# The Conformer convolution of a two-block decoder: 31 multiply-adds on VectorE, or matmuls over four shifts of 32 channels

## The chip, the cores and the metric

The kernel runs on one core of a Trainium2 chip, in float32. The metric is the device time of one execution in microseconds (us). TensorE (PE) does the matmuls, VectorE (DVE) and GpSimd (POOL) the elementwise work, ScalarE (ACT) the activations and most evictions, SyncE (SP) issues most of the DMAs from one queue that works in order.

## What is computed

Two blocks follow each other on 512 tokens of width 1024. The first is attention with a gated feed-forward; the second, on 528 rows (16 meta tokens ahead), has a Conformer branch, a bidirectional state-space branch (SSD) and 16 experts that each choose 66 tokens. The change is in the Conformer branch, cut here to what matters:

```python
def depthwise_conv(x, w, b):
    y = lax.conv_general_dilated(x, w[:, None, :].astype(x.dtype), window_strides=(1,), padding='SAME',
                                 dimension_numbers=('NWC', 'WIO', 'NWC'), feature_group_count=x.shape[-1])
    return y + b.astype(x.dtype)
...
        c = conf_a * jax.nn.sigmoid(conf_g)
        c = depthwise_conv(c, w_conf_dw[l], b_conf_dw[l])
        c = jax.nn.silu(layer_norm(c, conf_ln_g[l], conf_ln_b[l]))
        branch_conf = jnp.einsum('btc,cd->btd', c, w_conf_out[l])
```

The kernel of the convolution has 31 taps (`CONF_KERNEL`), each with its own weight for each of the 1024 channels; no channel mixes with another.

## The kernel before

Activations lie transposed: channels on the 128 partitions, the 528 rows along the free axis. A channel tile is 128 channels, so the Conformer branch has 8 of them (`KD`), the SSM input 24 (16 of `ys`, 4 of `Bt`, 4 of `Ct`), the gate `z` 16 and the branch gates 16.

**A linear tile.** `lin2h` makes one tile of 128 output channels in two halves of 264 columns (`HS`). SP loads the 512 KB of weights into `wraw` (L97, 3 buffers), ACT rounds them to `whi` (L107), POOL takes the rest to `wlo` (L108, 2 buffers each), and PE does three products for each of 8 slices of the contraction (L140 to L142): 48 matmuls of 264 columns.

**A Conformer tile.** `conf_tile(m, pl)` is two linear tiles. `gate_half` takes a tanh of the gate into `ct` (L887). `value_half` multiplies it with the value into `rcp`, which has 15 zeros on either side (L894). ACT does the first tap with the bias (L897); the other 30 taps are one `scalar_tensor_tensor` each on DVE, over all 528 columns, each adding to `co` (L900). They are not issued at once but put on the list `later`. The last one writes the tile to DRAM (`cfD`, L902).

**The order.** PE is scheduled by hand: it works in program order. The other engines' orders come from a scheduler. The program interleaves the pieces: for each of the four SSD groups `g`, `ssd_steps(g)` gives 16 steps, each with preparations (`pre`: on ACT, DVE, POOL) and matmuls (`mm`); between the steps stand the linear tiles of a list `fill` (the SSM convolutions of group g+1, z tiles, gate tiles, Conformer tiles by the table `CT`), and after each step `background(NB)` issues 6 taps, those of the SSM convolution first (`soon`, L749), then those of `later`. In the SSD steps `state_mm` (L806) and `y_mm` (L853) are the products, `M` (L830 to L833, 3 buffers for each direction) the decay matrix that `y_mm` waits for, and `row` a row broadcast from DRAM that SP loads (L817).

**After the groups** come the last four z tiles, the rest of `later`, the Conformer tile 7 from another pool (`lw`), five gate tiles, the sum of squares `ysp` with its reciprocal root (`rsqrt_mean`, L150 to L155), gate tile 15, the loads of `cfD` into `cf` (L1016) and the output products of the two branches.

Of the kernel before, what the change touches and what calls it, by code (L numbers as in the profile page):

```python
# [9 lines left out]
F32 = mybir.dt.float32  # L10
# [42 lines left out]
def lay_out_pv():  # L53
    n = 0
    for name, w in (("attn_g", 8), ("ffn_g", 8), ("dqg", 1), ("dkg", 1), ("sublng", 1), ("lam", 4),
                    ("mix_g", 8), ("cw", 248), ("cb", 8), ("lng", 8), ("lnb", 8), ("sw", 168), ("sb", 24),
                    ("dskip", 16), ("ssmg", 16), ("ffng2", 8), ("dtb", 1), ("alog", 1), ("slot", CAP), ("tid", 5)):
        PV[name] = (n, w)
        n += w
    return n  # L60
# [6 lines left out]
def body(ctx, tc, a, out):  # L67
# [58 lines left out]
    def V(name, i=0, n=1):  # L126
        o, w = PV[name]
        return pv[:, o + i:o + i + n]
# [498 lines left out]
    hv = b2p.tile([P, 24 + 248 + 8], F32, name="hv")  # L627
# [76 lines left out]
    pool.tensor_scalar(hv[:, 24:272], V("cw", 0, 248), 0.5, None, ALU.mult)  # L704
    pool.tensor_scalar(hv[:, 272:], V("lnb", 0, 8), 0.5, None, ALU.mult)
# [11 lines left out]
    soon, later = [], []  # L717

    def background(n):

        for _ in range(n):
            if soon:
                soon.pop(0)()
            elif later:
                q = later[0 if len(later) < 2 or len(later[0]) >= len(later[1]) else 1]
                q.pop(0)()
                if not q:
                    later.remove(q)
# [35 lines left out]
    def ssd_steps(g):  # L764
# [55 lines left out]
        def y_pre(c, q):  # L820
# [5 lines left out]
            for d in range(2):  # L826
                row = keep["row", c, q, d]
                M = ssp.tile([P, 4, P], F32, name=f"M{d}", tag=f"M{d}", bufs=3)
                for h in range(4):
                    act.activation(M[:n, h, :n], row[:n, h, :n], AF.Relu, scale=-1.0,  # L830
                                   bias=acsT[:n, c, 32 * d + H0 + h:32 * d + H0 + h + 1])
                act.activation(M[:n, :, :n], M[:n, :, :n], AF.Exp, scale=-1.0)
                dve.tensor_mul(M[:n, :, :n], M[:n, :, :n], cb[:n, d, :n].unsqueeze(1).to_broadcast([n, 4, n]))  # L833
                xd = ssp.tile([P, 256], F32, name=f"xd{d}", tag=f"xd{d}", bufs=2)
                pool.tensor_mul(h3(xd[:n]), h3(xT_[:n, c, 256 * q:256 * q + 256]), per_head(dtT, n, c, d, H0, 4))
                ops.append((xd[:n], M[:n]))
# [41 lines left out]
    cfD = dram.tile([P, KD, T], F32, name="cfD")  # L878

    def conf_tile(m, pl):  # L880

        th = []

        def gate_half():
            th.append(pl.tile([P, T], F32, name="ct", **(dict(tag="ct", bufs=1) if pl is ssp else dict(tag="tmp", bufs=3))))
            for ps, s0, s1 in lin2h(lambda i: W2[8 + m], U):
                act.activation(th[0][:, s0:s1], ps[:, :TH], AF.Tanh, scale=0.5)  # L887

        def value_half():
            rp = pl.tile([P, T + 30], F32, name="rcp", **(dict(tag="rcp", bufs=2) if pl is ssp else dict(tag="bs", bufs=NBS)))  # L890
            pool.memset(rp[:, :15], 0.0)
            pool.memset(rp[:, T + 15:], 0.0)
            for ps, s0, s1 in lin2h(lambda i: W2[m], U):
                dve.scalar_tensor_tensor(rp[:, 15 + s0:15 + s1], th[0][:, s0:s1], 1.0, ps[:, :TH], ALU.add, ALU.mult)  # L894
            o = pl.tile([P, T], F32, name="co", tag="co" if pl is ssp else "sq", bufs=2)
            cw = lambda k: hv[:, 24 + m * 31 + k:25 + m * 31 + k]
            act.activation(o, rp[:, :T], AF.Identity, bias=V("cb", m), scale=cw(0))  # L897

            def tap(k):
                dve.scalar_tensor_tensor(o, rp[:, k:k + T], cw(k), o, ALU.mult, ALU.add)  # L900
                if k == 30:
                    sp.dma_start(out=cfD[:, m, :], in_=o)  # L902

            later.append([lambda k=k: tap(k) for k in range(1, 31)])

        return [gate_half, value_half]

# [32 lines left out]
    CT = [(2,), (3,), (4, 5), (6,)]  # L940
# [8 lines left out]
    for f in conf_tile(0, ssp):  # L949
        f()  # L950
    dt_sums()
    for f in conf_tile(1, ssp):
        f()
    for g in range(4):
# [3 lines left out]
        ct = [f for m in CT[g] for f in conf_tile(m, ssp)]  # L958
        rest = [f for i in range(4) for c in (ct, zt, gt) for f in c[i:i + 1]]
# [20 lines left out]
        background(len(soon))  # L980
    for i in range(4):
        z_tile(12 + i)
# [9 lines left out]
    for m in (7,):  # L992
        for f in conf_tile(m, lw):
            f()
# [59 lines left out]
    for k in range(KD):  # L1054
# [3 lines left out]
        act.activation(th, t, AF.Tanh, bias=hv[:, 272 + k:273 + k], scale=0.5)  # L1058
        act.activation(t, t, AF.Identity, bias=hv[:, 272 + k:273 + k], scale=0.5)
# [471 lines left out]
def arrays_of(inp):  # L1531
# [18 lines left out]
    put("cw", g["w_conf_dw_2"][0].reshape(31, 8, P).transpose(2, 1, 0).reshape(P, 248))  # L1550
# [17 lines left out]
    r["w_ssm_out"] = pack_w(g["w_ssm_out_2"][0])  # L1568
    r["w_router"] = np.ascontiguousarray(g["w_router_2"][0].reshape(KD, P, 16).transpose(1, 0, 2))
# [31 lines left out]
```

## Time and profile before

| | |
|---|---|
| median of 3 runs | 2735.83 us (2733.57 to 2737.95) |
| the profiled execution | 2728.47 us, its span 2726.7 us |
| mean granted clock of TensorE | 0.958 |
| PE busy | 2444.2 us (90%) |
| DVE busy | 1546.9 us (57%) |
| ACT busy | 1091.7 us (40%) |
| POOL busy | 892.3 us (33%) |
| DVE's Conformer taps (L900) | 240 instructions, 286.6 us busy |

Times inside the execution count from the span's start. Busy time is the union of an engine's instructions, so matmuls that overlap count once, and a matmul at half the clock counts for longer than at the full one. The four groups of the SSD, with what is interleaved, lie between about 790 and 1360 us; this text calls that stretch the loop. What follows until about 1460 us is called the tail. The experts begin after 1680 us.

### The profile page before, as it was taken

Reading aid. Unit: us, or ns where it says so; the run is one execution under the profiler, and the core shown is the slowest. Engines: PE = TensorE matmul, PEld = TensorE weight load, DVE = VectorE, ACT = ScalarE, POOL = GpSimd, SP = SyncE. Lnnn points to the kernel's source line nnn. Section 1 sums busy time; section 2 is a strip of 40 time slices with the busy share of each in tenths; the row PEclk is TensorE's granted clock in tenths of the full one; section 3 lists DMA queues with packets and bytes.
Section 4 is the critical chain, followed back from the end, with each engine's and each line's share of the span. In section 5 each row is a group of like instructions: output and inputs, shape, how many; then the busy total and the mean of one; then the engine's idle time right before and its main releaser. Section 6 shows DMA issues by size and latency. Waiting matters only on the chain.

```text
span 2726.7 us, 63609 instructions
## 1 busy us (share of the span) xinstructions
PE 2444.2 (90%) x27884; PEld 2038.2 (75%) x27884; DVE 1546.9 (57%) x1913; ACT 1091.7 (40%) x1986; POOL 892.3 (33%) x650
## 2 busy tenths in 40 slices
PE   7999999999986788987798998899988898998897
PEld 6775678888875777885798997777767676776774
DVE  4426755532699999899866545344333333333335
ACT  5553532222453635463543422243333333333334
POOL 3543244444456657767644531000000000000000
PEclk9999999999988888998898999999999999999998
DMA  4111223333321323231324366999999999999996
GB/s 138 62 47 30 62 89 99 95 92 100 101 86 56 102 74 93 81 119 51 100 82 134 108 237 258 371 407 406 400 403 407 406 406 401 398 404 400 399 399 248
DMA packets 122834, 569.06 MB, mean 209 GB/s; under 512 B 23501, under 2 KB 23885, under 8 KB 73405
## 3 DMA queue, kind: packets, MB, share of 16 engines
q1 hardware_dynamic: 110832, 539.01, 52.6%
q10 hardware_dynamic: 8253, 17.53, 1.9%
q0 software_dynamic: 3472, 8.46, 1.3%
q8 instruction: 219, 3.59, 0.5%
q14 instruction: 58, 0.48, 0.1%
HBM read 545.64 MB, written 19.30 MB: 207 GB/s over the span
## 4 chain that ended last, share of the span: by engine, by line
PE 42%; DVE 24%; DMA 22%; issue 6%; ACT 4%; POOL 2%; ACTq 0%; DVEq 0%; SPq 0%; POOLq 0%
DVE co L900 9%; DMA eraw<-in_e_up_dram 8%; PE eg L1300 8%; DMA eraw<-in_e_down_dram 7%; DMA eraw<-in_e_gate_dram 6%; DVE ys L749 4%; PE fps L141 3%; PE fps L142 3%; PE fps L140 3%; DVE M L833 3%; PE lps L140 3%; PE lps L142 3%; PE lps L141 3%; PE l L140 2%; PE l L141 2%
## 5 line engine op out<-in xcount | busy, mean ns | idle before, releaser
L108 POOL TENSOR_TENSOR wlo<-wraw,whi 128x1024 fp32r<-128x1024 f32 (+2 forms) x212 | 500.0, 2359 | 511.8 <-ACT whi L107 474.5
L1300 PEld LDWEIGHTS eg<-x,eraw 128*64 128x64 f32 x16384 | 511.3, 138 | 144.7 <-issue 111.0
L1300 PE MATMUL eg<-x,eraw 128*64 128x66 f32 x16384 | 540.8, 224 | 85.4 <-issue 37.7
L107 ACT CAST whi<-wraw 128x1024 fp32r<-128x1024 f32 (+2 forms) x212 | 213.0, 1005 | 432.6 <-issue 233.4
L140 PE MATMUL l<-uh,wlo 128*128 128x264 f32 x1152 | 349.9, 304 | 32.1 <-POOL wlo L108 30.8
L1262 DVE TENSOR_TENSOR elo<-eraw,ehi 128x1024 fp32r<-128x1024 f32 x256 | 304.1, 1222 | 125.4 <-ACT ehi L1261 125.0
L141 PE MATMUL l<-ul,whi 128*128 128x264 f32 x1152 | 340.0, 295 | 0.0
L142 PE MATMUL l<-uh,whi 128*128 128x264 f32 x1152 | 339.2, 294 | 0.0
L900 DVE SCALAR_TENSOR_TENSOR co<-rcp,hv,co 128x528 f32<-128x528 f32 x240 | 286.6, 1201 | 13.0 <-ACT co L897 8.6
L1426 DVE TENSOR_TENSOR ht<-eg,hx 128x132 f32<-128x132 f32 x128 | 37.7, 295 | 439.4 <-PE eg L1300 439.4
L1261 ACT CAST ehi<-eraw 128x1024 fp32r<-128x1024 f32 x256 | 259.7, 1045 | 34.0 <-PE pd L142 24.6
L1271 POOL DMA_INDIRECT xg<-hnD,idx x16 | 15.9, 997 | 778.1 <-PE xtp L1288 591.8
L140 PEld LDWEIGHTS l<-uh,wlo 128*128 128x128 f32 x1152 | 231.3, 201 | 43.7 <-POOL wlo L108 37.8
L141 PEld LDWEIGHTS l<-ul,whi 128*128 128x128 f32 x1152 | 231.1, 201 | 1.3 <-issue 1.2
L142 PEld LDWEIGHTS l<-uh,whi 128*128 128x128 f32 x1152 | 229.9, 200 | 0.0
L140 PE MATMUL pd<-ehi,hl 128*66 128x512 f32 x512 | 211.6, 413 | 9.0 <-ACT ehi L1261 5.9
L141 PE MATMUL pd<-elo,hh 128*66 128x512 f32 x512 | 204.5, 399 | 0.8 <-DVE elo L1262 0.6
L142 PE MATMUL pd<-ehi,hh 128*66 128x512 f32 x512 | 204.3, 399 | 0.0
L1427 ACT CAST hh<-ht 128x132 fp32r<-128x132 f32 x128 | 38.7, 303 | 327.8 <-DVE ht L1426 327.8
L1424 ACT ACTIVATE hx<-eg 128x132 f32<-128x132 f32 x128 | 36.0, 281 | 294.9 <-PE eg L1300 294.9
L140 PE MATMUL fps<-hh,wlo 128*128 128x512 f32 x352 | 139.1, 395 | 0.9 <-POOL wlo L108 0.9
L141 PE MATMUL fps<-hl,whi 128*128 128x512 f32 x352 | 139.1, 395 | 0.1
(418 smaller groups left out, 4751.7 us busy)
## 6 DMA issues: line engine op xcount, KB each, us to landing
eraw<-in_e_gate_dram SPq DMA_DIRECT2D x128, 1024.0 KB
eraw<-in_e_up_dram SPq DMA_DIRECT2D x128, 1024.0 KB
eraw<-in_e_down_dram SPq DMA_DIRECT2D x126, 1024.0 KB
wraw<-in_w_in_dram SPq DMA_DIRECT2D x88, 512.0 KB
row<-rowD SPq DMA_DIRECT2D x64, 256.0 KB
wraw<-in_w_gate_dram SPq DMA_DIRECT2D x22, 512.0 KB
wraw<-in_w_up_dram SPq DMA_DIRECT2D x22, 512.0 KB
wraw<-in_w_down_dram SPq DMA_DIRECT2D x16, 512.0 KB
```

Of the source, the lines that this page charges most:

```text
L107: act.copy(hi[:, :e], raw[:, :e])
L108: pool.tensor_sub(lo[:, :e], raw[:, :e], hi[:, :e])
L140: pe.matmul(ps, sl, mh, start=first, stop=False)
L141: pe.matmul(ps, sh, ml, start=False, stop=False)
L142: pe.matmul(ps, sh, mh, start=False, stop=last)
L749: dve.scalar_tensor_tensor(dst, rp[:, k:k + T], V("sw", m * 7 + k), dst, ALU.mult, ALU.add)
L833: dve.tensor_mul(M[:n, :, :n], M[:n, :, :n], cb[:n, d, :n].unsqueeze(1).to_broadcast([n, 4, n]))
L900: dve.scalar_tensor_tensor(o, rp[:, k:k + T], cw(k), o, ALU.mult, ALU.add)
L1261: act.copy(hi, w[:, j, :])
L1262: dve.tensor_sub(lo, w[:, j, :], hi)
L1300: pe.matmul(ps[64 * h:64 * h + 64, j, :], w[:, k, P * j + 64 * h:P * j + 64 * h + 64], x[:, k, :], start=j == 0 and k == 0, stop=j == 1 an ...
L1427: act.copy(hid[0][:, s, :], ht)
```

## The change

The 31 taps become matmuls. `value_half` writes the padded tile `rcp` (now 559 columns) to a DRAM buffer `rcD`. A new function `conf_conv(m)` gives three pieces, `fetch(0)`, `taps(0)` and `taps(1)`:

- `fetch(h)`: for each block of 32 channels the tile is read back four times, each time one column further on, into 32 partitions of `cz` (four DMAs of 32x4x292). Partition 32 j + c of block b holds channel 32 b + c shifted by j. With the first half comes the weight tile `cw` (128x1024, 512 KB), whose 32x32 blocks are diagonal.
- `taps(h)`: for eight groups of four taps, and four blocks of 32 channels, one matmul of 128 rows, 32 output columns and 264 moving columns; the four blocks write to the partitions 0, 32, 64 and 96 of one PSUM tile. ACT evicts it with the bias. Then `taps(0)` issues `fetch(1)`, and `taps(1)` writes the tile to `cfD`.

`cz`, `cw`, `co` and `rcp` have one buffer each. `M` has 2 buffers in place of 3. The Conformer tile 7 moves into the loop, and all tiles come one place earlier (`CT`); the convolutions follow by a new table `CC`, with that of tile 7 among the last z tiles. The list `later` and the tap weights `cw` of the vector `pv` are gone.

```diff
-    hv = b2p.tile([P, 24 + 248 + 8], F32, name="hv")
+    hv = b2p.tile([P, 24 + 8], F32, name="hv")
...
-                M = ssp.tile([P, 4, P], F32, name=f"M{d}", tag=f"M{d}", bufs=3)
+                M = ssp.tile([P, 4, P], F32, name=f"M{d}", tag=f"M{d}", bufs=2)
...
+    rcD = dram.tile([KD, P, T + 31], F32, name="rcD")
...
-            rp = pl.tile([P, T + 30], F32, name="rcp", **(dict(tag="rcp", bufs=2) if pl is ssp else dict(tag="bs", bufs=NBS)))
+            rp = ssp.tile([P, T + 31], F32, name="rcp", tag="rcp")
             pool.memset(rp[:, :15], 0.0)
             pool.memset(rp[:, T + 15:], 0.0)
             for ps, s0, s1 in lin2h(lambda i: W2[m], U):
                 dve.scalar_tensor_tensor(rp[:, 15 + s0:15 + s1], th[0][:, s0:s1], 1.0, ps[:, :TH], ALU.add, ALU.mult)
-            o = pl.tile([P, T], F32, name="co", tag="co" if pl is ssp else "sq", bufs=2)
-            cw = lambda k: hv[:, 24 + m * 31 + k:25 + m * 31 + k]
-            act.activation(o, rp[:, :T], AF.Identity, bias=V("cb", m), scale=cw(0))
-
-            def tap(k):
-                dve.scalar_tensor_tensor(o, rp[:, k:k + T], cw(k), o, ALU.mult, ALU.add)
-                if k == 30:
-                    sp.dma_start(out=cfD[:, m, :], in_=o)
-
-            later.append([lambda k=k: tap(k) for k in range(1, 31)])
+            sp.dma_start(out=rcD[m], in_=rp)
...
+    def conf_conv(m):
+        o = []
+
+        def fetch(h):
+            s0, s1 = HS[h]
+            z = ssp.tile([P, 4, TH + 28], F32, name="cz", tag="cz")
+            for j in range(4):
+                sp.dma_start(out=z[32 * j:32 * j + 32],
+                             in_=rcD[m][:, s0 + j:s1 + j + 28].rearrange("(b c) t -> c b t", c=32))
+            if h == 0:
+                w = ssp.tile([P, 8, 4, 32], F32, name="cw", tag="cw")
+                sp.dma_start(out=w, in_=a["conf_dw"][m].rearrange("p (i b c) -> p i b c", i=8, b=4))
+                o.extend((ssp.tile([P, T], F32, name="co", tag="co"), w, None))
+            o[2] = z
+
+        def taps(h):
+            s0, s1 = HS[h]
+            ps = lin.tile([P, 512], F32, name="l3", tag="lin")
+            for i in range(8):
+                for b in range(4):
+                    pe.matmul(ps[32 * b:32 * b + 32, :TH], o[1][:, i, b, :], o[2][:, b, 4 * i:4 * i + TH],
+                              start=i == 0, stop=i == 7, skip_group_check=True)
+            act.activation(o[0][:, s0:s1], ps[:, :TH], AF.Identity, bias=V("cb", m), scale=0.5)
+            if h == 0:
+                fetch(1)
+            else:
+                sp.dma_start(out=cfD[:, m, :], in_=o[0])
+
+        return [lambda: fetch(0), lambda: taps(0), lambda: taps(1)]
...
-    CT = [(2,), (3,), (4, 5), (6,)]
+    CT = [(2,), (3, 4), (5, 6), (7,)]
+    CC = [(0, 1), (2,), (3, 4), (5, 6)]
...
-        ct = [f for m in CT[g] for f in conf_tile(m, ssp)]
-        rest = [f for i in range(4) for c in (ct, zt, gt) for f in c[i:i + 1]]
+        ct = [f for m in CT[g] for f in conf_tile(m)]
+        cc = [f for m in CC[g] for f in conf_conv(m)]
+        rest = [f for i in range(6) for c in (cc, ct, zt, gt) for f in c[i:i + 1]]
...
+    cc = conf_conv(7)
     for i in range(4):
+        if i < 3:
+            cc[i]()
         z_tile(12 + i)
...
-    for m in (7,):
-        for f in conf_tile(m, lw):
-            f()
```

What the change moves in the engines' instructions is shown at three places. Names: `yp` are SSD products, `l_...` a PSUM tile of a linear tile or of a convolution half, `cbp` the cross product of an SSD chunk, `row_...` the broadcast rows, `gD` the stored gates.

PE at the end of group 0, before: the last SSD steps with linear tiles between them.

```order
L853 MATMUL yp<-M_6694,xd_6701 64x16 x4
L853 MATMUL yp<-M_6703,xd_6710 64x16 x4
L853 MATMUL yp<-row_6524,pv_5873 64x16 x4
L788 MATMUL cbp<-Ct,Bt 128x128
L853 MATMUL yp<-M_6805,xd_6812 64x16 x4
L853 MATMUL yp<-M_6814,xd_6821 64x16 x4
L853 MATMUL yp<-row_6636,pv_5873 64x16 x4
L140 MATMUL l_6983<-uh,wlo 128x264
```

The same place in the change:

```order
L916 MATMUL l_7025<-cz,cw 32x264 x32
L847 MATMUL yp<-M_6901,xd_6908 64x16 x4
L847 MATMUL yp<-M_6910,xd_6917 64x16 x4
L847 MATMUL yp<-row_6703,pv_5871 64x16 x4
L782 MATMUL cbp<-Ct,Bt 128x128
...
L916 MATMUL l_7143<-cz,cw 32x264 x32
L847 MATMUL yp<-M_7080,xd_7087 64x128 x4
L847 MATMUL yp<-M_7089,xd_7096 64x128 x4
L847 MATMUL yp<-row_6897,pv_5870 64x128 x4
L916 MATMUL l_7197<-cz,cw 32x264 x32
```

The second half of tile 0 (`l_7025`) and both halves of tile 1 (`l_7143`, `l_7197`) now stand between these steps, each 32 matmuls, and no linear tile stands between them any more.

SP at the same place, before: rows, the two `cfD` writes and weight loads.

```order
L817 DMA row_6690<-rowD 128x512 [waits DMAHW6_49,DMAHW0_49,Activation_49]
L817 DMA row_6801<-rowD 128x512 [waits DMAHW7_49,DMAHW4_49,Activation_49]
L902 DMA cfD<-co 128x528 [waits DVE_49]
L817 DMA row_6692<-rowD 128x512 [waits DMAHW1_49,PE_49,Pool_49]
L97 DMA wraw<-in_w_in_dram 128x1024 [waits DMAHW2_49,Pool_49]
```

And in the change, from the last weight load ahead of the fetches:

```order
L97 DMA wraw<-in_w_in_dram 128x1024 [waits Pool_49]
L903 DMA cz<-rcD 32x4x292 [waits DMAHW3_49,PE_49]
L811 DMA row_7003<-rowD 128x512 [waits DMAHW4_49,PE_49]
L922 DMA cfD<-co 128x528 [waits DMAHW5_49,Activation_49]
L903 DMA cz<-rcD 32x4x292 [waits DMAHW6_49]
...
L907 DMA cw<-in_conf_dw_dram 128x1024 [waits DMAHW1_49]
...
L903 DMA cz<-rcD 32x4x292 [waits DMAHW6_49,DMAHW5_49,DMAHW7_49,DMAHW0_49,PE_49]
...
L903 DMA cz<-rcD 32x4x292 [waits DMAHW5_49,DMAHW6_49,DMAHW2_49,DMAHW7_49,DMAHW0_49,PE_49]
...
L97 DMA wraw<-in_w_in_dram 128x1024 [waits DMAHW1_49,Pool_49]
```

Three fetches that wait for PE, two of them with a weight tile, have come between two weight loads; the load ahead of them is the one for the fourth linear tile after `l_7256`, the next on PE.

DVE in the tail, before (`yl` is the low part of the split SSM output, `rs_m` the start of the reciprocal root):

```order
L900 SCALAR_TENSOR_TENSOR co<-rcp,hv,co 128x528
L136 SCALAR_TENSOR_TENSOR yl<-ys,pv,yh 128x528 x5
L900 SCALAR_TENSOR_TENSOR co<-rcp,hv,co 128x528 x29
L150 TENSOR_SCALAR rs_m<-ysp 128x264 x2
L153 TENSOR_TENSOR rs_l<-rs_r 128x528
```

In the change:

```order
L930 SCALAR_TENSOR_TENSOR zt<-zt,l_12287 128x264
L931 SCALAR_TENSOR_TENSOR ys<-ys,zt 128x528
L136 SCALAR_TENSOR_TENSOR yl<-ys,pv,yh 128x528 x16
L150 TENSOR_SCALAR rs_m<-ysp 128x264 x2
L153 TENSOR_TENSOR rs_l<-rs_r 128x528
```

The 29 taps of tile 7 that stood ahead of `rs_m` are gone.

## Rows read from the trace of the kernel before

**Rows 1.** Engines by stretch: the loop, its stretch without taps, the tail

```profile
core 0: us, PE busy (x) PEld busy (x) DVE busy (x) ACT busy (x) POOL busy (x), PEclk, DMA share, GB/s
790.00:1360.00 570.00, 455.22 (x3698) 409.27 (x3696) 534.68 (x589) 286.86 (x703) 391.31 (x301) 0.88 0.28 83
1090.00:1180.00 90.00, 81.85 (x660) 74.13 (x660) 79.56 (x81) 46.21 (x103) 68.94 (x52) 0.97 0.32 91
1360.00:1450.00 90.00, 86.79 (x699) 85.77 (x696) 62.42 (x65) 37.86 (x62) 36.92 (x19) 0.97 0.25 79
```

**Rows 2.** The same view of the Conformer taps (L900) alone: DVE busy, count, clock

```profile
790.00:1360.00 570.00, 243.51 (x198) 0.88 0.28 83
1090.00:1180.00 90.00, 2.81 (x3) 0.97 0.32 91
...
1180.00:1360.00 180.00, 110.50 (x90) 0.85 0.30 87
```

**Rows 3.** The chain of waits that ended last, by line (page, part 4)

```profile
DVE co L900 9%; DMA eraw<-in_e_up_dram 8%; PE eg L1300 8%; DMA eraw<-in_e_down_dram 7%; DMA eraw<-in_e_gate_dram 6%; DVE ys L749 4%; PE fps L141 3%; PE fps L142 3%; PE fps L140 3%; DVE M L833 3%; PE lps L140 3%; PE lps L142 3%; PE lps L141 3%; PE l L140 2%; PE l L141 2%
```

**Rows 4.** Whom PE waited for in the loop: us, times, longest

```profile
PE yp L853 <- DVE M L833: 36.1, 14, 5.4
PE l L140 <- POOL wlo L108: 23.9, 13, 4.8
PE stp L806 <- POOL xe L798: 17.8, 6, 6.9
```

**Rows 5.** The taps by line (page, part 5): count, busy us, mean ns

```profile
L900 DVE SCALAR_TENSOR_TENSOR co<-rcp,hv,co 128x528 f32<-128x528 f32 x240 | 286.6, 1201 | 13.0 <-ACT co L897 8.6
```

**Rows 6.** Timeline of PE, a linear tile at full clock: start us, us

```profile
1340.83 0.28 PE L140 MATMUL l<-uh,wlo 128*128 128x264 f32 x1
1340.95 0.29 PE L141 MATMUL l<-ul,whi 128*128 128x264 f32 x1
1341.08 0.28 PE L142 MATMUL l<-uh,whi 128*128 128x264 f32 x1
```

**Rows 7.** Timeline: one float32 product of 264 columns, two instructions

```profile
698.23 0.61 PE L584 MATMUL nps<-sqa,cst 128*128 128x264 f32 x2
```

**Rows 8.** Groups by line, 690 to 1410 us: that line's mean ns

```profile
L584 PE MATMUL nps<-sqa,cst 128*128 128x264 f32 x4 | 1.2, 385 | 0.0
```

**Rows 9.** Timeline: 128 expert products of 66 columns in two column groups

```profile
1903.49 4.33 PE L1300 MATMUL eg<-x,eraw 128*64 128x66 f32 x128
```

**Rows 10.** Those products by line (page, part 5): count, busy us, mean ns

```profile
L1300 PE MATMUL eg<-x,eraw 128*64 128x66 f32 x16384 | 540.8, 224 | 85.4 <-issue 37.7
```

**Rows 11.** Timeline of PE: from 128 output columns to 64 and back

```profile
1343.63 0.28 PE L142 MATMUL l<-uh,whi 128*128 128x264 f32 x1
1343.84 0.64 PE L853 MATMUL yp<-M,xd 16*64 16x16 f32 x16
...
1346.08 0.39 PE L140 MATMUL l<-uh,wlo 128*128 128x264 f32 x1
1346.31 0.28 PE L141 MATMUL l<-ul,whi 128*128 128x264 f32 x1
```

**Rows 12.** Timeline: SP issues loads of 264 KB, and DVE's first use

```profile
1453.77 1.40 SPq L1016 DMA_DIRECT2D cf<-cfD  x3
...
1458.96 1.05 DVE L1035 TENSOR_TENSOR mu<-cf 128x528 f32<-128x528 f32 x1 [2.35 <-DMA cf<-cfD]
```

**Rows 13.** Timeline of the tail on DVE, ACT, POOL, PE; in brackets idle time before

```profile
1420.71 31.64 DVE L900 SCALAR_TENSOR_TENSOR co<-rcp,hv,co 128x528 f32<-128x528 f32 x29
1452.27 0.76 DVE L150 TENSOR_SCALAR rs_m<-ysp 128x264 f32<-128x264 f32 x2
...
1453.07 0.64 ACT L151 ACTIVATE rs_l<-rs_m 128x528 f32<-128x528 f32 x1 [11.40 <-DVE rs_m L150]
...
1457.10 2.35 POOL L108 TENSOR_TENSOR wlo<-wraw,whi 128x1024 fp32r<-128x1024 f32 x1 [14.96 <-ACT whi L107]
...
1459.50 0.59 PE L140 MATMUL l<-yh,wlo 128*128 128x264 f32 x1 [8.68 <-POOL wlo L108]
```

**Rows 14.** What SP's queue waited for, 690 to 1480 us: us, times, longest

```profile
SPq L97 <- POOL wlo L108: 512.9, 74, 24.2
```

More of the change, by code (lines that the diff above doesn't have):

```diff
@@ L55, in lay_out_pv @@
     for name, w in (("attn_g", 8), ("ffn_g", 8), ("dqg", 1), ("dkg", 1), ("sublng", 1), ("lam", 4),
-                    ("mix_g", 8), ("cw", 248), ("cb", 8), ("lng", 8), ("lnb", 8), ("sw", 168), ("sb", 24),
+                    ("mix_g", 8), ("cb", 8), ("lng", 8), ("lnb", 8), ("sw", 168), ("sb", 24),
                     ("dskip", 16), ("ssmg", 16), ("ffng2", 8), ("dtb", 1), ("alog", 1), ("slot", CAP), ("tid", 5)):
@@ L703, in body @@
     pool.tensor_scalar(hv[:, :24], V("sb", 0, 24), 0.5, None, ALU.mult)
-    pool.tensor_scalar(hv[:, 24:272], V("cw", 0, 248), 0.5, None, ALU.mult)
-    pool.tensor_scalar(hv[:, 272:], V("lnb", 0, 8), 0.5, None, ALU.mult)
+    pool.tensor_scalar(hv[:, 24:], V("lnb", 0, 8), 0.5, None, ALU.mult)
     first = [[(lin.tile([P, 512], F32, name="l3", tag="lin"), s0, s1) for s0, s1 in HS] for _ in range(2)]
@@ L715, in body @@
     dt_softplus(first[0])
-    soon, later = [], []
+    soon = []
     def background(n):
@@ L723, in background @@
                 soon.pop(0)()
[L724 to L728, printed above, removed]
     def conv_ssm(tiles, first=None):
@@ L878, in body, with conf_tile @@
     cfD = dram.tile([P, KD, T], F32, name="cfD")
-    def conf_tile(m, pl):
+    rcD = dram.tile([KD, P, T + 31], F32, name="rcD")
+    def conf_tile(m):
         th = []
         def gate_half():
-            th.append(pl.tile([P, T], F32, name="ct", **(dict(tag="ct", bufs=1) if pl is ssp else dict(tag="tmp", bufs=3))))
+            th.append(ssp.tile([P, T], F32, name="ct", tag="ct", bufs=1))
             for ps, s0, s1 in lin2h(lambda i: W2[8 + m], U):
@@ L948, in body @@
     background(len(soon))
-    for f in conf_tile(0, ssp):
+    for f in conf_tile(0):
         f()
     dt_sums()
-    for f in conf_tile(1, ssp):
+    for f in conf_tile(1):
         f()
@@ L1057, in body @@
         dve.scalar_tensor_tensor(t, t, V("lng", k), rsc, ALU.mult, ALU.mult)
-        act.activation(th, t, AF.Tanh, bias=hv[:, 272 + k:273 + k], scale=0.5)
-        act.activation(t, t, AF.Identity, bias=hv[:, 272 + k:273 + k], scale=0.5)
+        act.activation(th, t, AF.Tanh, bias=hv[:, 24 + k:25 + k], scale=0.5)
+        act.activation(t, t, AF.Identity, bias=hv[:, 24 + k:25 + k], scale=0.5)
         dve.scalar_tensor_tensor(t, th, 1.0, t, ALU.add, ALU.mult)
@@ L1549, in arrays_of @@
     put("mix_g", cols(g["w_norm_mix_2"][0]))
-    put("cw", g["w_conf_dw_2"][0].reshape(31, 8, P).transpose(2, 1, 0).reshape(P, 248))
     put("cb", cols(g["b_conf_dw_2"][0]))
@@ L1568, in arrays_of @@
     r["w_ssm_out"] = pack_w(g["w_ssm_out_2"][0])
+    w = np.concatenate([g["w_conf_dw_2"][0], np.zeros((1, D), np.float32)]).reshape(8, 4, 8, 4, 32).transpose(2, 1, 4, 0, 3)
+    cw = np.zeros((8, 4, 32, 8, 4, 32), np.float32)
+    for c in range(32):
+        cw[:, :, c, :, :, c] = w[:, :, c]
+    r["conf_dw"] = cw.reshape(8, P, 1024)
     r["w_router"] = np.ascontiguousarray(g["w_router_2"][0].reshape(KD, P, 16).transpose(1, 0, 2))
```

## The prediction

> **What bounds the kernel now.** I read the chain of waits first. Its lines name the Conformer taps on DVE before anything else: 9% of the span, some 245 us [rows 3]. All 240 taps together are busy 286.6 us, so most of them lie on the chain [rows 5]. Next come the engines by stretch. In the loop (790 to 1360 us) DVE is busy 534.68 of 570 us, 243.51 of them with 198 taps [rows 1, 2]. PE is busy 455.22, so it idles 114.8 us, and its granted clock is 0.88: it loses by waiting and by running at the lower of its two levels (1.2 and 2.4 GHz). The reader should see that these two losses are all that can be won there.
>
> How PE does without taps is shown by 1090 to 1180 us, where three taps ran: it is busy 81.85 of 90 us (9% idle) at clock 0.97, although DVE is still busy 79.56 us [rows 1, 2]. In the tail, with z and gate tiles only, it idles 3.6% (86.79 of 90) [rows 1]. PE's longest waits in the loop are for `M` from DVE (36.1 us) and `wlo` from POOL (23.9 us) [rows 4]: DVE's queue works in order, and the taps stand ahead of `M`. From about 1680 us the experts run, which the change doesn't touch; I let what is won earlier reach the end in full.
>
> **The change, part by part.**
>
> *Taken from DVE.* 198 taps in the loop, 243.51 us; 534.68 - 243.51 leaves it 291 us. This is no gain by itself; it takes the cause from PE's idle time. ACT gives up eight first taps and gets sixteen evictions of half the width: the same number of elements, costed at nothing because ACT is busy only 286.86 of 570 us [rows 1]; were it full, it would still be an exchange of equals.
>
> *PE's present work at full clock.* A clock of 0.88 means 24% of the 570 us at half speed, 137 us. If all 114.8 us of idle time lie in that, only 22 us of work ran at half speed, and the work is 455 - 11 = 444 us; if none do, it is 455 - 68 = 387. I take the middle, 416.
>
> *Added to PE.* One float32 product of 264 columns is two instructions in 0.61 us, of which the last one's own 0.385 comes after the start of that one: 0.225 us apart [rows 7, 8]. A tile of the new convolution has 64 products, 128 instructions: 28.8 us if they ran one after another. No row shows four column groups; the nearest has two. There 128 instructions of 66 columns take 4.33 us; without the last one's 0.224 that is 32.4 ns each, where one alone would need 66/264 of 225, so 56.3, and two at a time 28.1 [rows 9, 10]. The groups thus run side by side, with 4.2 ns lost per instruction. For 264 columns and four groups: 225/4 + 4.2 = 60.5 ns, 7.8 us per tile. The ends are 7.2 us (four-fold, nothing lost) and 28.8 us; I take 7.8, by the row it comes from.
>
> The Trainium skill, page "TensorE: Matmul & The Clock Gate", Part 3 (packing small matmuls), gives 3.07-fold for four row tiles and 2.38-fold for three column tiles. By its 3.07, as an estimate, a tile takes 9.4 us and the gain is 13 us smaller; no run here shows it.
>
> The loop gets seven of the eight convolutions, 54.6 us. It also gets the two linear tiles of Conformer tile 7: 2 x 48 matmuls at 0.122 us are 11.7 us [rows 6]. Going from 128 output columns to fewer and back costs 0.21 and 0.23 us where 0.12 is usual [rows 11], so 0.2 us for each of 14 halves, 2.8 us. Together 69 us: 416 + 69 = 485.
>
> *PE's idle share.* At least one stretch shows 9%, with DVE nearly full of SSM taps; the tail shows 3.6%. In the changed loop DVE is little more than half busy, but the SSD steps with their chains through ACT, DVE and POOL stay, and `M` with two buffers can be made only one step ahead. I take 7%: 485/0.93 = 521.5 us. If the third `M` buffer was needed, part of the 36.1 us stays [rows 4]; the upper end covers that.
>
> *Fetches.* A fetch waits until PE has left `cz`, and PE then waits for the data. By PE's order this is bare at four places, where no linear tile stands between two halves: both halves of tile 1 in group 0, and the second halves of tiles 4 and 6. Loads of 264 KB take 5.2 us from issue to use, behind other loads [rows 12]; a fetch half brings 584 KB in four DMAs, a first half 512 KB of weights besides. At most 4 x 5.2 = 21 us. From below no row excludes that the short state products between them hide it all, so 0; I take 15. The other fetches have a linear tile (48 x 0.122 = 5.9 us) or more in front. Loop: 521.5 + 15 = 536.5 in place of 570, **-33.5 us**.
>
> *SP's queue.* It gets 8 writes of `rcD`, 64 DMAs of the fetches and 8 weight loads, about 16 MB. Over some 540 us that is 30 GB/s on top of 83, at a DMA share of 0.28 [rows 1]: costed at nothing. Weight loads queue behind fetches that wait for PE, but they wait for `wlo` anyway, 512.9 us in all [rows 14], and the order has the weights of four more linear tiles asked for ahead of those fetches, 23 us of PE work. The one `rcp` buffer waits for its write to DRAM; a gate half of 5.9 us lies between.
>
> *The tail.* DVE runs 29 taps of tile 7 for 31.6 us until 1452.3; `rs_m` stands behind them, ACT waits 11.40 us for it, the cast of the next weights stands behind that, POOL waits, and PE idles 8.68 us [rows 13]. The taps are gone, the chain is short, and gate tile 15 covers it: -8.7. If the table loads now come late instead, a few us return. The two linear tiles leave, -11.7; convolution 7 comes, +7.8 and 0.4 for its switches. **-12.2 us.**
>
> *Sum.* -33.5 - 12.2 = -45.7 us. Against the profiled execution, 2728.47, that is 2682.8. The median of the runs is 2735.83, 7.4 above it; I take the same difference from that: **2690 us**. The runs spread by 4.4 us; 0.2% (5.5 us) is what a measurement of this kernel can tell from no change.
>
> **The rivals.**
>
> *A, more is won.* If the idle share falls to the tail's 3.6%, the work is the lower 387 us and fetches cost 5: (387 + 69)/0.964 + 5 = 478, -92 - 12 = -104, 2632 us. For it: in the last group 90 taps keep DVE busy 110.5 of 180 us [rows 2], and there the SSM convolutions are over. Against: the SSD steps' chains stay.
>
> *B, the column groups overlap less (slower than before).* Place: the 32 matmuls of each half. The two instructions of one product follow each other on the same column group. If only neighbours overlap, four groups run no better than two: 14.4 + 0.6 = 15 us per tile, 8 x 7.2 = 58 us more than forecast, 2748. One after another it would be 8 x 21 = 168 more, 2858. It decides from 7.8 + 45.7/8 = 13.5 us per tile, 105 ns per instruction. For it: two groups are all that rows show. Against: two groups lose little, even with short products. The same Part 3 states that matmuls start strictly in program order and that a weight load overlaps a running matmul only in another row group; that would give B. The trace speaks against the second half: all 128 rows are used, and 32.4 ns leaves no room for a load between products [rows 9].
>
> *C, SP's queue stalls PE.* If each of the 15 fetches after the first, rather than four, is exposed for 5.2 us, that is 78 in place of 15 us: 2753. It decides once fewer than two linear tiles' weights are ready when SP gets past a fetch. Against it: the four tiles of lead.
>
> *D, the taps were only filling.* POOL (391 of 570 us) and the SSD chains hold the loop at 570 us whatever DVE does; only the tail gains: 2724. For it: POOL is busy 68.94 of 90 us where the taps are absent. Against: there PE idles only 9% [rows 1].
>
> **How the numbers follow.** Forecast 0.50, with its own range 2658 to 2723: lower end with 400 us of work and 5% idle, (400 + 69)/0.95 + 10 = 504, so -66 - 12, 2658; upper end with 430 us, 9% and 21 us of fetches, (430 + 69)/0.91 + 21 = 569, so -1 - 12, 2723. A 0.12, B 0.20, C 0.08, D 0.10. The range runs from 2645, which leaves out the far half of A (0.06), to 2757, which takes in two-group B, D and C at its price and leaves out B in full and what of C is worse (0.12). Faster by over 0.2%: 0.50 + 0.12 + 0.07 of D + 0.04 of B where part of it hides = 0.73. Within 0.2%: 0.03 of B and 0.03 of D, 0.06. Slower: the other 0.13 of B, and C, 0.21.
>
> **What would show it.** The convolution's matmuls should start about 60 ns apart at full clock, 7 to 8 us per tile; 110 ns or more is B. DVE in the loop falls to 55% or less, the granted clock rises above 0.93, and the wait of `yp` for `M` shrinks. Waits of the convolution for the DMA `cz` should appear at four places, 2 to 5 us each; at most halves, it is C. The 8.68 us before the first SSM product go. If the loop still takes 570 us with DVE half idle, my reason is wrong and D is right.

## The result, and the profile after

| | before | after |
|---|---|---|
| median of 4 runs | 2734.7 us (2728.36 to 2737.95) | 2688.57 us (2687.11 to 2690.77) |
| the profiled execution, its span | 2728.47, 2726.7 us | 2687.14, 2685.4 us |
| mean granted clock of TensorE | 0.958 | 0.974 |

The changed kernel is faster: the ratio of the times is 0.9832, 95% interval 0.9817 to 0.9847, or -46.1 us. The forecast was 2690.

To see where the time went, three marks are read: the first linear tile, the last SSD product, and the sums behind the loop. The first linear tile on PE's timeline before (start, duration):

```profile
707.76 0.48 PE L140 MATMUL l<-uh,dtl 128*64 128x264 f32 x1
```

The SSD products by line before (duration in ns, then first and last start):

```profile
L853 PE MATMUL yp<-row,pv x512: 209/273/421, 849.2 to 1368.6; 128*64 128x128 f32 x149, 128*64 128x16 f32 x22
```

The first linear tile on the timeline after:

```profile
717.35 0.48 PE L140 MATMUL l<-uh,dtl 128*64 128x264 f32 x1 [2.17 <-ACT uh L604]
```

And the SSD products by line after:

```profile
L847 PE MATMUL yp<-row,pv x512: 209/273/323, 852.5 to 1331.7; 128*64 128x128 f32 x149, 128*64 128x16 f32 x22
```

From the first linear tile to the last SSD product it took 660.8 us and takes 614.3: **-46.5**. The code ahead of 700 us is the same in both but for a smaller table of vectors, so the 9.6 us by which the second execution comes later there are taken as no part of the change. Most of them come between 200 and 400 us, where the granted clock is 0.98 before, 0.94 after, and 0.95 in e1_no_taps, which is built on the kernel before; in the runs below that mark lies anywhere from 708 to 719, at 715 and 716 in two built on the kernel before. Two of the 9.6 us belong to the mark itself: PE waits ahead of it after (2.17 us), behind it before (3.06). Counted from the tile's next product (711.30 and 718.80) the loop's gain is 44.4 us. The tail, to the Conformer's mean (`mup`, at 1479.5 and 1431.2), took 110.9 us and takes 99.5: **-11.4**. From there to the first expert product it is +3.9, the experts +3.1. Together 9.6 - 46.5 - 11.4 + 3.9 + 3.1 = -41.3, the difference of the two spans.

The engines by stretch after, for [rows 1]; the second line is the loop itself, first SSD transposes to last SSD product (the columns are those of that group):

```profile
790.00:1360.00 570.00, 527.19 (x5109) 461.73 (x5108) 343.61 (x410) 308.08 (x747) 375.86 (x314) 0.96 0.40 118
804.00:1332.00 528.00, 485.61 (x4704) 423.55 (x4703) 334.85 (x397) 290.56 (x711) 360.80 (x304) 0.95 0.39 117
```

DVE fell from 534.68 to 343.61 busy us in the same 570 (the last 28 of them belong to the tail in the changed kernel), PE rose from 455.22 to 527.19, and the clock from 0.88 to 0.96. Whom PE waited for in the loop, for [rows 4]:

```profile
PE l L916 <- DMA cz<-rcD: 14.7, 4, 5.7
PE l L140 <- POOL wlo L108: 10.9, 5, 4.8
PE l L916 <- DMA row<-rowD: 9.1, 1, 9.1
```

The 36.1 us of `yp` for `M` are gone; the new waits are those of the convolution for its fetches.

The timeline of PE shows the convolution by halves of 64 instructions (start, duration, in brackets the idle time before). First one at full clock, then the four behind a bare fetch:

```profile
1337.89 3.77 PE L916 MATMUL l<-cz,cw 128*32 128x264 f32 x64
...
909.62 6.45 PE L916 MATMUL l<-cz,cw 128*32 128x264 f32 x64 [9.12 <-DMA row<-rowD]
...
920.93 5.46 PE L916 MATMUL l<-cz,cw 128*32 128x264 f32 x64 [3.39 <-DMA cz<-rcD]
...
1220.72 6.21 PE L916 MATMUL l<-cz,cw 128*32 128x264 f32 x64 [5.27 <-DMA cz<-rcD]
...
1325.41 5.08 PE L916 MATMUL l<-cz,cw 128*32 128x264 f32 x64 [5.65 <-DMA cz<-rcD]
```

Twelve of the 16 halves are like the first line: four instructions start within 20 ns and the next four 0.224 us later, 16 times; that is 3.6 us for a half and 7.2 us for a tile (over the 63 gaps, a mean of 53.7 ns). The other four come behind the idle time of a fetch and then take 1.3 to 2.7 us longer, partly at the lower level of the clock: granted 0.57, 0.69, 0.60 and 0.73 in these halves, 1.00 in the first line's. By stretch, the first slow half and that one:

```profile
909.62:916.07 6.45, 6.45 (x66) 3.22 (x68) 0.73 (x1) 0.00 (x0) 0.18 (x1) 0.57 0.07 24
...
1337.89:1341.66 3.77, 3.77 (x66) 2.05 (x65) 2.26 (x2) 1.34 (x2) 2.37 (x1) 1.00 0.00 0
```

All four stand where the prediction expected bare fetches.

The tail by stretch, before (last SSD product to `ysp`, then to `mup`):

```profile
1368.60:1438.10 69.50, 66.29 (x534) 65.81 (x529) 50.01 (x49) 33.01 (x56) 34.25 (x18) 0.98 0.30 96
1438.10:1479.50 41.40, 32.72 (x247) 32.38 (x246) 23.96 (x31) 11.25 (x14) 16.34 (x8) 0.88 0.47 156
```

After:

```profile
1331.70:1401.20 69.50, 62.83 (x566) 59.09 (x563) 28.82 (x30) 30.73 (x52) 24.81 (x12) 0.95 0.33 106
1401.20:1431.20 30.00, 30.00 (x246) 29.87 (x245) 12.11 (x15) 11.36 (x14) 17.02 (x8) 1.00 0.61 202
```

All of the tail's gain is in its second part, where PE has no idle time left (8.68 us before, [rows 13]). In the first part two linear tiles left and one convolution came, and yet it is as long: PE now idles 6.7 us there in place of 3.2. The waits of PE in that part after:

```profile
PE l L140 <- ACT gt L943: 6.2, 1, 6.2
```

### The profile page after: what moved, and what is told of

Read it like the earlier page. It is cut to its first block, busy times and chain, and to the rows that moved or that the text cites. A ratio compares the mean times of both kernels' runs of the same rounds, so it can differ in the third digit from the quotient of the medians.

```text
span 2685.4 us, 65619 instructions
## 1 busy us (share of the span) xinstructions
PE 2470.9 (92%) x28908; PEld 2044.1 (76%) x28908; DVE 1302.6 (49%) x1673; ACT 1096.7 (41%) x1997; POOL 856.2 (32%) x649
## 4 chain that ended last, share of the span: by engine, by line
PE 53%; DMA 29%; DVE 8%; issue 5%; POOL 2%; ACT 2%; SPq 0%; DVEq 0%; ACTq 0%; POOLq 0%
DMA eraw<-in_e_down_dram 10%; DMA eraw<-in_e_up_dram 9%; DMA eraw<-in_e_gate_dram 8%; PE eg L1320 6%; PE l L140 6%; PE l L142 5%; PE l L141 5%; PE fps L141 3%; PE fps L142 3%; PE fps L140 3%; PE lps L140 3%; PE lps L142 3%; PE lps L141 3%; PE l L916 2%; PE yp L847 2%
## 5 line engine op out<-in xcount | busy, mean ns | idle before, releaser
L140 PE MATMUL l<-uh,wlo 128*128 128x264 f32 x1152 | 341.6, 297 | 21.0 <-POOL wlo L108 14.8
L142 PE MATMUL l<-uh,whi 128*128 128x264 f32 x1152 | 333.1, 289 | 0.0
L141 PE MATMUL l<-ul,whi 128*128 128x264 f32 x1152 | 332.4, 289 | 0.0
L140 PEld LDWEIGHTS l<-uh,wlo 128*128 128x128 f32 x1152 | 223.0, 194 | 29.6 <-POOL wlo L108 24.5
L141 PEld LDWEIGHTS l<-ul,whi 128*128 128x128 f32 x1152 | 223.1, 194 | 1.9 <-issue 1.4
L142 PEld LDWEIGHTS l<-uh,whi 128*128 128x128 f32 x1152 | 222.6, 193 | 0.0
L142 PE MATMUL fps<-hh,whi 128*128 128x512 f32 x352 | 138.4, 393 | 0.0
```

The costliest lines, as they stand in the source:

```text
L140: pe.matmul(ps, sl, mh, start=first, stop=False)
L141: pe.matmul(ps, sh, ml, start=False, stop=False)
L142: pe.matmul(ps, sh, mh, start=False, stop=last)
```

## The experiments

My theory: DVE's queue works in order, and the taps in it held PE back; the change takes that away and pays with PE time for the products and with bare fetches. The rivals: PE was held by something else; the column groups overlap whatever the order; the price of the change lies in SP's queue. Ratios below are to the kernel before, run on the same chip. Differences to the changed kernel are between medians of different sessions; the kernel before had 2733 to 2736 us in them, so 3 us say nothing there.

**e1_no_taps** is the kernel before, without the taps:

```diff
-            later.append([lambda k=k: tap(k) for k in range(1, 31)])
+            sp.dma_start(out=cfD[:, m, :], in_=o)
```

> The kernel before, with the 30 multiply-adds of every tile on DVE left out (only the first tap, ACT's, is computed), and nothing put on PE: the whole relief without its price. Theory (DVE's in-order queue holds PE back by its idle time and by the lower clock that follows): the loop of about 577 us shortens to PE's present work at full clock with 7% idle, 416/0.93 = 447 us, and the taps of tile 7 no longer stand ahead of the sums behind the loop (-8.7): 2736 - 130 - 9 = about 2597 us, 2585 to 2615; granted clock in the loop over 0.93, no wait of yp for M. Rival (the loop has a second bound close behind DVE: ACT, POOL or the weights): over 2650 us, with the clock still under 0.93.

Measured: 2612.45 us, ratio 0.9548 (0.953 to 0.9565), -123.5 us by that ratio and -120.9 by the two medians. Its loop by stretch:

```profile
800.00:1264.00 464.00, 426.93 (x3754) 390.30 (x3752) 325.44 (x394) 288.24 (x705) 360.83 (x299) 0.96 0.34 102
```

PE's longest waits in that stretch:

```profile
PE l L140 <- POOL wlo L108: 14.4, 10, 3.9
PE xtp L778 <- ACT xTt L779: 10.6, 4, 6.1
PE stp L806 <- POOL xe L798: 4.6, 2, 4.4
PE yp L853 <- DVE M L833: 3.8, 3, 3.2
```

The theory stands so far: the taps held PE back. The wait for `M` falls from 36.1 to 3.8 us. The loop ends at 464 us, not at 447; the longest waits are now those for POOL's `wlo` and ACT's `xTt`. The change keeps 46 of these 121 to 124 us; the other 75 to 77 are its price.

**e1b_no_taps7** leaves out the taps of tile 7 alone (`if m < 7:` before the line above).

> The kernel before, with the 30 multiply-adds of tile 7 alone left out, those behind the loop; its two linear tiles stay where they were. Theory (the PE idle of 8.7 us behind the loop is owed to these taps standing on DVE ahead of the sums that PE needs): 2735 - 9 = 2726 us, 2722 to 2730. Rival (the idle is owed to ACT's evictions or splits there): 2733 to 2737.

Measured: 2726.95 us, ratio 0.9969 (0.9957 to 0.9982), -8.5 us by that ratio and -6.4 by the two medians. The tail by stretch:

```profile
1376.10:1445.60 69.50, 66.32 (x534) 65.83 (x531) 32.50 (x34) 33.07 (x56) 33.64 (x18) 0.98 0.31 100
1445.60:1475.70 30.10, 30.10 (x247) 29.96 (x246) 11.80 (x15) 11.37 (x14) 17.23 (x8) 1.00 0.62 204
```

The second part falls from 41.4 to 30.1 us as in the changed kernel, the first stays. So the tail's gain of 11.4 us is that of these 30 taps alone, and more than their 8.7 us of idle time, since the clock there rises from 0.88 to 1.00 as well.

**e5_M2** is the kernel before with `bufs=2` for `M`.

> The kernel before with two buffers of M in place of three, a part of the change that frees room. Theory (M is made late because DVE's multiply that finishes it stands in DVE's queue, not for want of a buffer): no change, 2731 to 2739 us. Rival (M is asked for one step ahead only as far as buffers go, and the third is used): the 36 us in which yp waits for M grow, 2745 to 2760 us.

Measured: 2737.32 us, ratio 1.0014 (1.0003 to 1.0025), +3.8 us. PE's longest wait in the loop:

```profile
PE yp L853 <- DVE M L833: 53.3, 21, 7.6
```

The time is the theory's, the wait the rival's. The wait grows by 17 us, but the time by 3.8 only: what PE waits longer for `M` it waits less elsewhere, for `xe` 12.2 in place of 17.8 us, for ACT's `xTt` 14.2 in place of 20.7, for DVE's `ys` nothing in place of 9.7.

**e8_both** puts DVE work back into the changed kernel, on a scratch tile:

```diff
+    junk = ssp.tile([P, 440], F32, name="junk", tag="junk")
...
             sp.dma_start(out=rcD[m], in_=rp)
+            if m < 7:
+                later.append([lambda: dve.scalar_tensor_tensor(junk, junk, V("cb", m), junk, ALU.mult, ALU.add) for _ in range(36)])
```

> The changed kernel with as much DVE work put back as the taps took: 36 multiply-adds of 440 columns on a scratch tile behind each of tiles 0 to 6, in the same background places, which nobody waits for but what stands behind them on DVE. Theory (DVE's queue was the bound): DVE in the loop is 335 + about 244 = 579 us, at the busy share that it had before (534 of 577) a loop of about 620 us in place of 528: 2689 + 92 = about 2780 us, 2755 to 2800; yp waits for M again, 25 us or more; clock under 0.92. Rival (the gain came from PE's denser work alone, or from what stands elsewhere in the order): 2685 to 2705 us.

Measured: 2792.19 us, ratio 1.0208 (1.0189 to 1.0226), 103.6 us above the changed kernel. The added instructions are all done at 1161 us; the loop by stretch up to there and behind it:

```profile
822.00:1161.00 339.00, 244.76 (x2152) 209.69 (x2151) 334.31 (x397) 136.16 (x335) 184.02 (x151) 0.85 0.29 85
1161.00:1437.00 276.00, 256.90 (x2546) 224.36 (x2545) 163.03 (x206) 153.21 (x375) 190.40 (x153) 0.97 0.41 118
```

PE's longest waits in the whole loop:

```profile
PE yp L854 <- DVE M L834: 32.9, 12, 10.6
PE l L140 <- POOL wlo L108: 18.6, 8, 5.7
PE btp L782 <- DVE ys L859: 17.7, 1, 17.7
```

The time comes back. DVE is busy 497 of 615 us (81%; I had expected 579, but these instructions were shorter than the taps), but that is the mean of two unlike stretches: where the added instructions stand it is busy 334.31 of 339 us (99%), and of the 64 us in which PE waits for DVE (`M`, `ys` and 13.0 for `zt`) 63 lie there. Behind them PE waits 0.4 us for `M`. So DVE work that PE doesn't need holds PE back, but this run does not tell DVE's sum of work, full in that stretch, from the place of that work in the queue. Rows of the kernel before point both ways: from 791.5 to 990 us DVE is busy 195.7 of 198.5, from 1270 to 1368.6 only 82.58 of 98.6, and there too PE waits 15.8 us for `M`. A run that moves the taps behind `M` and keeps their sum was not made.

**e3_swap** and **e4_pairs** change only the order in which a half's 32 matmuls are issued: each group's eight in a row, or two groups at a time.

```diff
-            for i in range(8):
-                for b in range(4):
+            for b in range(4):
+                for i in range(8):
```

```diff
+            for i, b in [(i, p + b) for p in (0, 2) for i in range(8) for b in range(2)]:
```

> The changed kernel with the two loops of the taps exchanged: each column group does its 8 products in a row before the next group begins. In the changed kernel 64 instructions of a half take 3.77 us at full clock, four groups side by side. If the side by side needs the groups to alternate: 64 times about 0.21 us = 13.4 us for a half, 10 us more for each of 16 halves, less what falls into PE's idle time: 2689 + 140 = about 2830 us, 2790 to 2860. If the groups run apart whatever the order: 3.8 us a half and 2685 to 2695 us.

> The changed kernel with two column groups at a time: groups 0 and 1 alternate through their 8 products, then groups 2 and 3. Theory (products of different groups that are issued next to one another overlap, as many as alternate): half the overlap, 64 times about 0.107 us = 6.9 us for a half, 3.1 us more for each of 16 halves: 2689 + 50 = about 2739 us, 2720 to 2745, which is near the time before, the break-even that the prediction put at 105 ns for an instruction. Rival (overlap doesn't depend on the order): 2685 to 2695 us.

Measured: e3_swap 2804.64 us, ratio 1.024 (1.0223 to 1.0258); e4_pairs 2717.99 us, ratio 0.9934 (0.9916 to 0.9952). A half at full clock on PE's timeline in e4_pairs:

```profile
1155.52 6.46 PE L916 MATMUL l<-cz,cw 128*32 128x264 f32 x64
```

The same in e3_swap:

```profile
1191.14 11.85 PE L916 MATMUL l<-cz,cw 128*32 128x264 f32 x64
```

And two stretches of 1 us inside that half, with the line's own instructions alone (PE busy with the count running in it, weight loads, clock, DMA):

```profile
1192.20:1193.20 1.00, 1.00 (x7) 0.47 (x5) 1.00 0.06 16
1193.80:1194.80 1.00, 1.00 (x10) 0.57 (x9) 1.00 0.00 0
```

The overlap hangs on the order: 3.77, 6.46 and 11.85 us for a half with four, two and one group at a time (53.7, 96.4 and 181.9 ns per instruction). One group at a time is quicker than 64 x 0.22 = 14.1 us, as the last two rows show: most of the time one instruction starts every 0.22 us, but where a group ends twice as many start, because the next group begins when three of the former group's instructions have yet to start. From e4_pairs to e3_swap the kernel loses 86.7 us, as much as 85.5 ns on 1024 instructions make (87.6); from the changed kernel to e4_pairs only 29 of 44 us. Break-even with the kernel before lies some 18 us above e4_pairs, at about 114 ns; the prediction said 105.

**e7_one_tap** keeps one of the eight steps: `range(8)` becomes `range(1)`.

> The changed kernel with one of the eight steps of taps (4 of 32 taps) in each half, the other seven left out; the fetches, evictions and the order stay. It measures what the conv's products cost on the path. Theory (PE is on the path nearly throughout, so their time counts in full): a half falls from 3.8 to 6.5 us (mean about 4.3) to about 0.6, 16 times 3.7 = 59 us: about 2630 us, 2620 to 2645. Rival (the products fill gaps in which PE would have waited anyway): over 2660 us.

Measured: 2642.37 us, ratio 0.9654 (0.9636 to 0.9673), -46 us where the products left out took 56 (12 halves by 3.1 us and the four slow ones by 4.7). Four fifths of PE's time for them counts; the waits for the fetches stay (12.3 for `cz` and 6.3 for `cw`), and behind the loop the last half, which waited 0.4 us, now waits 4.3.

**e2_spread** deals the pieces of the convolution evenly among the others of a pass:

```diff
-        rest = [f for i in range(6) for c in (cc, ct, zt, gt) for f in c[i:i + 1]]
+        rest = [f for i in range(6) for c in (ct, zt, gt) for f in c[i:i + 1]]
...
+        no = len(fill)
+        for i in reversed(range(len(cc))):
+            fill.insert(i * no // len(cc), cc[i])
```

> The changed kernel with the pieces of the conv (fetch, first half, second half) spread evenly among the linear tiles and the short convolutions of a pass, so that no half stands right behind its fetch. Theory (the four bare places cost their waits for cz, 14.3 us, the wait for row that lies in the same queue, 9.1, and about 8 us of half-clock work behind them): the loop is 24 to 32 us shorter: about 2661 us, 2655 to 2672, and no wait of L916 for cz over 2 us. Rival (covering the fetches only moves the idle time to the next late thing, wlo or row): 2680 to 2692 us.

Measured: 2650.78 us, ratio 0.969 (0.9656 to 0.9724), 38 us below the changed kernel by the medians and 33 by the two profiled spans. The loop by stretch:

```profile
799.00:1300.00 501.00, 480.81 (x4753) 424.04 (x4752) 320.52 (x397) 297.22 (x724) 360.10 (x307) 0.99 0.43 126
```

PE's longest waits there:

```profile
PE yp L847 <- DVE M L827: 8.1, 5, 3.8
PE xtp L772 <- ACT xTt L773: 3.5, 4, 1.7
```

Every half now takes 3.77 us, the convolution waits 0.6 us in all, and the clock is 0.99. So the four bare fetches cost 14.3 + 9.1 us of waiting (the fifth wait, of 0.4 us, lies in the tail) and 8.1 us at the lower clock (96.3, 80.5, 92.5 and 74.6 ns from start to start in place of 53.7, over 63 gaps each), 31.5 us, and next to nothing took their place: one linear tile (some 6 us) has moved from ahead of the loop into it, so the loop alone shows less; from the first linear tile to the last SSD product it takes 581 us in place of 614.

**e2b_actq** issues the same fetches from ACT's queue in place of SP's (`act.dma_start`), the order of the pieces as in the changed kernel.

> The changed kernel with only the conv's fetches (cz and cw) issued from ACT's queue in place of SP's; the order of the pieces stays, so the four bare places stay bare. Theory (a bare fetch costs its flight, about 4.3 us, and the 9.1 us wait was longer because row, cfD and cw stand between the pieces in SP's queue): the four waits of about 14.7 us stay, the 9.1 us wait shrinks to about 4: 2689 - 5 = about 2684 us, 2678 to 2690. Rival (SP's queue is most of the waits): under 2672 us. Other rival (the issues and their waits for a free cz hold up ACT's evictions): over 2692 us.

Measured: 2699.84 us, ratio 0.9865 (0.9839 to 0.9892), 11 us above the changed kernel. By the number the second rival holds, and the first is out: the long wait became longer, now for `cw`, as PE's timeline has it:

```profile
913.22 1.11 PE L916 MATMUL l<-cz,cw 128*32 128x264 f32 x8 [10.69 <-DMA cw<-in_conf_dw_dram]
```

The rows show its reason the other way round, though: the fetch stood behind ACT's activations of `M`. Its first DMA went out 3.4 us after the start of the eviction of the half that had used the tile, by ACT's timeline:

```profile
900.36 0.48 ACT L918 ACTIVATE co<-l,pv 128x264 f32<-128x264 f32 x1 [2.35 <-PE l L916]
900.74 1.56 ACT L824 ACTIVATE M<-row,acsT 128x128 f32<-128x128 f32 x5
...
903.78 0.31 ACTq L903 DMA_DIRECT2D cz<-rcD  x1
```

ACT's queue is no cure; work between fetch and use is.

**e9_spread_gates** is e2_spread with the 16 splits behind the loop dealt out between the gate tiles:

```diff
-    for m in range(NG, 15):
-        gate_tile(m, lw)
+    for j in range(16):
+        if j < 15 and j % 3 == 0:
+            gate_tile(NG + j // 3, lw)
+        split_scaled(yh[j // 8][:, j % 8, :], yl[j // 8][:, j % 8, :], ys[:, j, :], V("ssmg", j))
```

> The version with the conv's pieces spread evenly, and behind the loop the 16 splits of ys on ACT, which stood in one piece ahead of five gate tiles, now stand three at a time between them. Theory (PE's wait of 6.3 us for ACT's gate eviction there is owed to the splits ahead of it in ACT's queue, and it lies on the path): 2650.8 - 6 = about 2645 us, 2640 to 2648, and no wait of L140 for gt over 1 us. Rival (the time behind the loop is set by what follows, the splits' second halves on DVE or the sums): 2649 to 2653 us.

Measured: 2647.62 us, ratio 0.9669 (0.9646 to 0.9693). The tail's first part by stretch:

```profile
1298.90:1362.60 63.70, 61.43 (x567) 57.24 (x562) 29.62 (x32) 32.59 (x55) 28.44 (x14) 1.00 0.33 100
```

PE's longest wait in it:

```profile
PE l L140 <- POOL wlo L108: 1.7, 1, 1.7
```

The wait for `gt` is gone and the part is 5.2 us shorter than e2_spread's 68.9. In the whole time it shows as 3 us, inside the two intervals, so it is not told apart from e2_spread. By its median it is the fastest version that leaves nothing out: 89 us below the kernel before, 41 below the change.

## Why the prediction was right

The direction and the size were right, the time within 2 us of the median. Step by step:

- **The taps on DVE hold PE back**: right, shown from both sides by e1_no_taps and e8_both. Rival D, with the loop staying at 570 us, is out. That they do so by standing ahead of `M`, rather than by filling DVE, is argued and not shown: e8_both doesn't separate the two. One sign was missed: DVE was to fall to 55% of the loop or less and is at 60% of the same 570 us (343.61).
- **PE's present work at full clock, 416 us**: e1_no_taps' loop has 426.93 us of PE work at clock 0.96, so between 408 and 427. Right.
- **The convolution, 7.8 us per tile**: measured 7.2, the lower end: four groups overlap in full, and the 4.2 ns lost per instruction that I took from the two-group row [rows 9] don't appear. The Trainium skill's 3.07-fold ("TensorE: Matmul & The Clock Gate", Part 3) would have given 9.4; the 53.7 ns are four-fold. Rival B, and the rule beside it, did not decide here, but B's place and point were right: with two groups at a time e4_pairs is near break-even, with one e3_swap is slower than before.
- **The idle share, 7%**: too much. Of the 528 us PE idles 42.4, and 23.4 of these are the fetches; the rest is 19 us or 3.6%, where I took 36.5. That is rival A's share. What kept A's 2632 us away are the fetches (32 us by the next point, 5 in A) and the work (408 us or more, 387 in A). It is also the share that I read from the tail, but those 90 us were no stretch of z and gate tiles only: they hold the two linear tiles of tile 7 as well, and taps on DVE.
- **The fetches, 15 us, at most 21**: the four places were right, the price was not. The waits alone are 23.4 us: the first half of tile 1 waits 9.12, not 5.2, behind five DMAs that SP could issue only when `cz` came free, with `row` and `cfD` between them. SP's queue on the timeline there, after:

```profile
898.31 0.32 SPq L903 DMA_DIRECT2D cz<-rcD  x1
899.21 0.32 SPq L811 DMA_DIRECT2D row<-rowD  x1
899.63 0.37 SPq L922 DMA_DIRECT2D cfD<-co  x1
900.04 2.83 SPq L903 DMA_DIRECT2D cz<-rcD  x3
902.93 0.42 SPq L907 DMA_DIRECT2D cw<-in_conf_dw_dram  x1
903.94 4.34 SPq L811 DMA_DIRECT2D row<-rowD  x3
```

  The queue's order need not be the cause. In the same stretch the 16 DMA engines are busy throughout (share 1.01, at 300 GB/s), where I had costed the traffic at nothing by the loop's mean share of 0.28:

```profile
898.30:909.60 11.30, 2.19 (x50) 1.90 (x51) 4.77 (x10) 8.37 (x23) 4.70 (x6) 0.64 1.01 300
```

  e2b_actq, from another queue, waited 10.69 us at this place; which of the two makes a bare first half so long is not shown. And I left out that PE works at the lower clock behind such a wait, 8.1 us more. Together 32 us: e2_spread confirms it. This error of 17 us and that of the idle share, 18 us, nearly cancel; that the forecast came so near is partly luck. The rest of the loop's surplus (-46.5 against -33.5) is the convolution (4 us) and a remainder of some 8 us: two come of the mark, the others lie within the bounds of PE's work but were not measured as such.
- **SP's queue costs nothing elsewhere**: rival C did not occur; eleven halves found their data, and the last, in the tail, waited 0.4 us.
- **The tail, -12.2**: measured -11.4, by another sum. The taps of tile 7 gave 11.3, not 8.7 (e1b_no_taps7). The exchange of two linear tiles for a convolution, which I put at -3.5, gave nothing: their cover gone, PE waited 6.2 us for ACT's `gt`, behind 16 splits in ACT's queue. e9_spread_gates shows that wait can be had back.
- **The experts' stretch in full**: the 3.9 us before the experts were not foreseen. They show in every kernel built on the change (214 to 216 us from `mup` to the first expert product, 210 to 211 in those built on the kernel before), with the same code and a lower clock there. In the ten us from 190.5 us behind `mup` the clock is 1.00 before (PE busy 5.57 us) and 0.66 after (8.08). Why it falls earlier there stays open.

## What to carry to other kernels

An engine that is busy 94% of a stretch can hold another back with work that nobody waits for yet. Look at it by parts, since a mean hides a stretch at 99%, and price the removal by the waiter's idle time and clock. When work moves to the engine that waited, put other work between each of its transfers and their use; here four uncovered fetches took 32 us, two thirds of what the change won, and three lines of ordering gave it back. Small matmuls for different column groups must alternate in program order, or most of the overlap is lost.

## What was not expected of the hardware

- Four column groups of 32 ran side by side with nothing lost: 53.7 ns per instruction of 264 columns, where one group starts one every 0.22 us.
- By the starts in the trace, PE begins an instruction for a free column group ahead of earlier ones that wait for a busy group: in e3_swap the next group begins when three of the former have yet to start, in e4_pairs the next pair when three of each of two groups have. The records don't name the group; the reading rests on the starts and on the half's 11.85 us in place of 14.1. The page of the Trainium skill named above (Part 3) has matmuls start and end strictly in program order; these rows differ.
- A wait of 3 to 9 us can cost more than itself: the halves behind the four fetches took 1.3 to 2.7 us longer at a lower clock. Not every wait does: in e3_swap a half behind 3.48 us took the usual 11.85.
